# Five of seven head projections of a dilated mixer moved into seven-product block units

## The chip, the cores and the metric

The kernel runs on one core of a Trainium2 chip. The metric is the device time of one execution in microseconds (us), lower is better. A core has a matrix engine (TensorE, in the profile PE, with its weight loads as PEld), a vector engine (VectorE, DVE), an engine for functions of one argument (ScalarE, ACT), a general engine (GpSimd, POOL) and an engine that here only issues transfers (SyncE, SP). Each works through its own queue in order; semaphores order them among each other. TensorE writes to PSUM, of which the kernel uses eight banks: two under the name pj, six under the name at. All else lies in SBUF or in DRAM. Transfers (DMAs) are issued from the queues of SP, ACT and POOL and run beside the engines.

## The reference

One layer of a decoder trunk over 512 tokens and 2048 channels. The input is normalised and modulated to u, and one wide projection of u gives the columns of three token mixers (A: differential attention, B: retention, C: dilated windows) and of their gates. Of C, which the change is about, this is computed for 8 heads of width 128 and three groups (window, dilation) = (128,1), (512,4), (2048,16):

```
proj = einsum('bsd,de->bse', u, w_in)          # c_q, c_k, c_v: 3 groups x 8 heads x 128 columns each
s = einsum(qs * dh ** -0.5, kk); s = where(valid, s, -inf)     # per group and head
lse = logsumexp(s); p = exp(s - lse); o = einsum(p, vv)
o = sum over groups of softmax(lse over groups) * o
y_c = (o * silu(c_z)) @ P_c
merged = sigmoid(g_a) * y_a + sigmoid(g_b) * y_b + sigmoid(g_c) * y_c
x = x + gate(c) * (merged @ W_out), then a last rms_norm
```

All is float32. A product of two float32 matrices is made of three TensorE products of rounded parts: each operand is split into a high part (rounded, "h") and a low part (the rest, "l"), and hh, hl and lh are summed in PSUM (`mm3`, L157 to L160). The high part is a copy on ACT, the low part a subtraction, nearly always on DVE.

## The kernel before

Tokens lie on the free axis: u is held as 16 tiles of 128 channels by 512 tokens, split into `uh` and `ul`. The work runs in stages one after another: a start (modulation, normalisation, raw gate columns), a stage of block units, then mixer C with its gate phase, mixer A with its gate phase, mixer B with its gate phase, the output projection.

**A plain projection**, `proj` (L162), makes 128 columns for all 512 tokens. Its weights come in two halves of 1024 by 128 (`w_load`, a 512 KB DMA on SP; `w_half`, the ACT copy at L146 and the DVE subtraction at L147), through a ring of three buffers each for the raw, high and low parts (wr, wh, wl). Each half gives 24 products of 512 columns, 48 for a projection. A function `mid` can be called between the halves; in stage C it carries the attention work of a step before.

**A block unit**, `unit_jobs` (L555), makes 1024 columns of the same projection with the seven products of Strassen's scheme (Winograd's form) over a 2 by 2 division of tokens, channels and columns, where the direct way has eight. It is a list of 14 jobs: two each for P1, P2 and R3 ("plain" jobs, weights as they are) and eight for the four products of weight sums ("sum" jobs). A job loads 1 MB of weights to an xr tile (three buffers), in a sum job makes four additions on DVE (L592), splits it (`x_split`: ACT at L506, DVE at L507; two buffers for xh and xl), and multiplies. With `fm=True` the weights are stationary and 256 tokens move, so a job is 48 products of 256 columns and the result has channels on partitions; else it is 24 products of 512 columns. The loop at L676 loads for job i+2, splits for job i+1 and multiplies job i; the split of job i+1 needs the buffer that job i-1 leaves, so its ACT copy begins as job i begins. Nine units run: five for values (v of C's three groups, of A and of B; written to `v_dram`), four for the gates of A and B (`fm=True`; an ACT sigmoid, then written by POOL's queue). The order of this stage is that of the text where `pin` is called.

**Stage C** (L942 to L976) runs for each head seven plain projections: q and k of the three groups, and z, the gate path. Results are split from PSUM (`split` L177, `split_pairs` L196) and consumed within the head: `first_scores` (group 1: products, mask and row minimum on DVE, exp on ACT, statistics sent through DRAM), `first_turn` (seven transposes and a split), `scores(1)` and `scores(2)` (the dilated groups, which see the tokens in the order of `perm`), and, held over to the next head, `turn` (eight transposes and a split), `values` (products with v, evacuation), `weigh` on POOL and `finish`. v is loaded every second head for two heads by `v_load` (L210) through the ring of the weights. The bias of C's gate (a weighted column sum of the gate weights, 9 blocks) is built on POOL at one block or so per head by `gate_bias_load` (L707), with its own DMAs on POOL's queue, and finished by a single small product (`gate_bias_sum`, L722).

The order of the instructions on each queue outside pinned text is made by the framework's scheduler from the text's order and the times at which operands are ready, so work after a `mid` may be put before it. Buffers with `bufs=1` make a writer wait for the last reader of the old content.

Of the kernel before, what the change touches and what calls it, by code (L numbers as in the profile page):

```python
# [17 lines left out]
P = 128  # L18
S = 512
# [45 lines left out]
def hybrid_kernel(ctx, tc, x, c, w_in, w_pa, w_pb, w_pc, w_out, w_ada, b_ada, norm_w, lam,  # L65
# [32 lines left out]


# [34 lines left out]

    def w_half(src, k0, c0, rot=False, tiles=None, low=dve):

        r, h, l = tiles or w_load(src, k0, c0)
# [7 lines left out]
        else:  # L145
            act.copy(h, r)  # L146
            low.tensor_sub(l, r, h.bitcast(F32))  # L147
        return h, l

    pinned = [False]  # L150

    def pin(instr):

        if pinned[0]:
            tc.keep_in_program_order(instr)
# [40 lines left out]
    def split_pairs(pool, tag, src):  # L196

        t = pool.tile([P, 4, 2, P], F32R, tag=tag, name=tag)
        act.copy(t[:, :, 0, :], src)
        dve.tensor_sub(t[:, :, 1, :], src, t[:, :, 0, :].bitcast(F32))  # L200
        return t
# [353 lines left out]
    def unit_jobs(w, c0, put, fm=False, early=False):  # L555
# [4 lines left out]
        def pure_load(k0, cc):  # L560
            r = wxp.tile([P, 4, 512], F32, tag="xr", name="xr", bufs=3)
            nc.sync.dma_start(out=r, in_=w[k0:k0 + 512, cc:cc + 512].rearrange("(j p) c -> p j c", p=P))
            return r
# [21 lines left out]
        def sum_load(j):  # L585
            r = wxp.tile([P, 4, 512], F32, tag="xr", name="xr", bufs=3)
            for i in range(2):
                nc.sync.dma_start(out=r[:, 2 * i:2 * i + 2, :],
                                  in_=w[(i * HJ + j) * P:(i * HJ + j + 1) * P, c0:c0 + 1024]
                                  .rearrange("p (a c) -> p a c", a=2))  # L590
# [59 lines left out]
    def put_gates(g, b0):  # L650
        def put(t, half, cc):
            def f():
# [6 lines left out]


    units = [unit_jobs(w_in, c0, put_values(unit), early=unit == 3)
             for unit, c0 in ((2, C_V), (3, C_V + 1024), (4, C_V + 2048), (0, A_V), (1, B_V))]
    units += [unit_jobs(w_in, g + b0 * P, put_gates(g, b0), fm=True) for g in (G_A, G_B) for b0 in (0, 8)]
    jobs = units[1][0] + units[0][0] + units[0][1] + units[1][1]
# [26 lines left out]
    pinned[0] = False  # L691
    for f in later:
        f()
    for f in deferred:
        f()
    wx_es.close()
# [3 lines left out]
    wp_es, wp = open_pool("wp2", "left", reuse_waits="tile")  # L700
# [5 lines left out]

    def gate_bias_load(pool, db):  # L707
        br = pool.tile([P, P], F32, tag="br", name="br", bufs=2)
        for q in range(4):
            r = pool.tile([P, 4, P], F32, tag="bw", name="bw", bufs=1)  # L710
            nc.gpsimd.dma_start(out=r, in_=w_in[q * 512:(q + 1) * 512, G_C + db * P:G_C + (db + 1) * P]
                              .rearrange("(j p) c -> p j c", p=P))
            nc.gpsimd.tensor_mul(r, r, sh[:, q * 4:q * 4 + 4].unsqueeze(2).broadcast_to([P, 4, P]))
            nc.gpsimd.tensor_add(r[:, 0:2, :], r[:, 0:2, :], r[:, 2:4, :])
            if q == 0:
                nc.gpsimd.tensor_add(br, r[:, 0, :], r[:, 1, :])
            else:
                nc.gpsimd.tensor_add(r[:, 0, :], r[:, 0, :], r[:, 1, :])
                nc.gpsimd.tensor_add(br, br, r[:, 0, :])
        return br  # L720

    def gate_bias_sum(db, br):  # L722
# [83 lines left out]
    bias_todo, bias_open = list(range(NF + NM)), []  # L806

    def bias_step():
        while bias_open:
            gate_bias_sum(*bias_open.pop(0))  # L810
        bias_more()

    def bias_more():
        if bias_todo:
            db = bias_todo.pop(0)
            bias_open.append((db, gate_bias_load(cp, db)))

# [4 lines left out]
    def c_head(hd, e1, e23, st, p0):  # L822
# [3 lines left out]
        def first_scores(qh, ql, kc):  # L826
# [504 lines left out]
```

## Time and profile before

| what | us |
|---|---|
| median of 3 runs (2663.86 to 2667.76) | 2665.14 |
| the profiled execution's own time | 2663.64 |
| its span, first to last instruction | 2661.9 |
| stage of block units, first to last product, about | 723 |
| stage C up to its gate phase, about | 681 |
| mean granted TensorE clock over the span | 0.989 |

The page lists each engine's busy time; its chain of waits, followed back from the end, says which engine held the end up at each moment. Products overlap in the pipeline, so the duration of one (some 0.39 us for 512 columns) is longer than the distance from one start to the next, and the cost of a product is that distance. The answer by windows gives busy times in a chosen stretch, from the span's start.

### The profile page before, as it was taken

To read this page: it belongs to the slowest core of one execution; us is meant where nothing else is said; L and a number is where in the kernel's file an instruction comes from. 1 tells how busy PE (TensorE), PEld (TensorE's weight loads), DVE (VectorE), ACT (ScalarE), POOL (GpSimd) and SP (SyncE) were. 2 spreads that over 40 slices of the span, in tenths; PEclk is the share of its full clock that TensorE was granted. 3 is DMA by queue.
4 is the path that set the end of the run, shared out by engine and by line. 5 is a ranking of instruction groups with operands and counts; after the bars stand their busy time and mean duration, and the time that the engine had idled before them with its cause. 6 is when DMAs were issued, how large, how long until landed. Compare 5 with 4: busy or idle time off the path is not lost.

```text
span 2661.9 us, 33296 instructions
## 1 busy us (share of the span) xinstructions
PE 2568.5 (96%) x13091; PEld 2184.6 (82%) x13091; DVE 1689.0 (63%) x2427; ACT 1058.6 (40%) x1431; POOL 269.6 (10%) x271
## 2 busy tenths in 40 slices
PE   6999999999999999999999999999999989999898
PEld 5777778888999988888888888788888768878778
DVE  7994888777778754444443444357667457676674
ACT  4233433333334433233333333246666235653222
POOL 3332000000000024122214200000000000000000
PEclk9999999999999999999999999999999999999999
DMA  9776666666666655344445443542333563336862
GB/s 345 252 273 227 231 208 226 225 221 214 197 207 220 208 154 147 96 119 120 114 119 123 106 121 109 175 142 82 93 88 92 171 194 104 98 99 210 299 222 103
DMA packets 414017, 449.47 MB, mean 169 GB/s; under 512 B 24786, under 2 KB 308132, under 8 KB 412708
## 3 DMA queue, kind: packets, MB, share of 16 engines
q1 hardware_dynamic: 384388, 396.91, 47.6%
q0 software_dynamic: 9760, 33.59, 4.2%
q10 hardware_dynamic: 19712, 16.85, 1.9%
q8 instruction: 102, 1.67, 0.3%
q14 instruction: 55, 0.45, 0.1%
HBM read 406.86 MB, written 40.44 MB: 168 GB/s over the span
## 4 chain that ended last, share of the span: by engine, by line
PE 74%; DVE 11%; DMA 8%; ACT 3%; issue 2%; SPq 0%; POOL 0%; ACTq 0%; DVEq 0%
PE pj L158 15%; PE pj L160 15%; PE pj L159 15%; PE at L159 8%; PE at L160 8%; PE at L158 8%; DVE acc L318 3%; DMA gpr<-part 2%; DMA gwa<-in_w_ada_dram 1%; DVE xl L507 1%; DMA gsg<-g 1%; DMA xr<-in_w_in_dram 1%; DMA part<-gsg 1%; DMA xr<-ud 1%; DVE xr L592 1%
## 5 line engine op out<-in xcount | busy, mean ns | idle before, releaser
L158 PE MATMUL pj<-uh,wh 128*128 128x512 f32 x1552 | 611.9, 394 | 7.1 <-ACT wh L146 4.8
L160 PE MATMUL pj<-uh,wl 128*128 128x512 f32 x1552 | 608.0, 392 | 7.3 <-DVE wl L144 4.6
L159 PE MATMUL pj<-ul,wh 128*128 128x512 f32 x1552 | 606.7, 391 | 0.0
L147 DVE TENSOR_TENSOR wl<-wr,wh 128x1024 fp32r<-128x1024 f32 x226 | 287.0, 1271 | 392.0 <-ACT wh L146 364.6
L146 ACT CAST wh<-wr 128x1024 fp32r<-128x1024 f32 x228 | 239.2, 1051 | 516.7 <-PE pj L159 365.7
L506 ACT CAST xh<-xr 128x2048 fp32r<-128x2048 f32 x126 | 240.7, 1910 | 365.0 <-PE at L160 152.5
L507 DVE TENSOR_TENSOR xl<-xr,xh 128x2048 fp32r<-128x2048 f32 x126 | 288.8, 2292 | 125.4 <-ACT xh L506 124.6
L160 PEld LDWEIGHTS pj<-uh,wl 128*128 128x128 f32 x1552 | 292.5, 188 | 70.3 <-DVE wl L144 5.5
L158 PEld LDWEIGHTS pj<-uh,wh 128*128 128x128 f32 x1552 | 293.0, 189 | 65.1 <-ACT wh L146 5.0
L159 PEld LDWEIGHTS pj<-ul,wh 128*128 128x128 f32 x1552 | 292.8, 189 | 58.1
L592 DVE TENSOR_TENSOR xr<-xr 128x512 f32<-128x512 f32 x288 | 198.8, 690 | 12.3 <-DMA xr<-in_w_in_dram 5.1
L158 PE MATMUL at<-yh,wh 128*128 128x512 f32 x336 | 131.8, 392 | 5.9 <-DVE gsg L777 5.0
L159 PE MATMUL at<-yl,wh 128*128 128x512 f32 x336 | 131.5, 391 | 0.0
L160 PE MATMUL at<-yh,wl 128*128 128x512 f32 x336 | 131.5, 391 | 0.0
L160 PE MATMUL at<-fh,xl 128*128 128x256 f32 x384 | 108.9, 284 | 0.7 <-DVE xl L507 0.7
L158 PE MATMUL at<-fh,xh 128*128 128x256 f32 x384 | 108.7, 283 | 0.0
L159 PE MATMUL at<-fl,xh 128*128 128x256 f32 x384 | 108.7, 283 | 0.0
L158 PE MATMUL at<-wh,mh 128*128 128x512 f32 (+1 forms) x256 | 93.1, 369 | 6.2 <-DVE res L1252 3.8
L159 PE MATMUL at<-wl,mh 128*128 128x512 f32 (+1 forms) x256 | 94.9, 371 | 0.2
L160 PE MATMUL at<-wh,ml 128*128 128x512 f32 (+1 forms) x256 | 94.5, 369 | 0.0
L278 POOL TENSOR_TENSOR wl<-wr,wh 128x896 fp32r<-128x896 f32 x32 | 77.3, 2421 | 136.5 <-ACT wh L277 127.3
L159 PE MATMUL at<-xl,fh 128*128 128x512 f32 x224 | 88.8, 396 | 2.1 <-DVE xl L507 1.8
(419 smaller groups left out, 5035.4 us busy)
## 6 DMA issues: line engine op xcount, KB each, us to landing
wr<-in_w_in_dram SPq DMA_DIRECT2D x196, 512.0 KB, 3.9
xr<-in_w_in_dram SPq DMA_DIRECT2D x144, 512.0 KB, 4.5
xr<-in_w_in_dram SPq DMA_DIRECT2D x54, 1024.0 KB, 5.1
wa<-in_w_ada_dram SPq DMA_DIRECT2D x20, 1024.0 KB, 9.1
wr<-in_w_out_dram SPq DMA_DIRECT2D x32, 512.0 KB, 4.6
gwa<-in_w_ada_dram SPq DMA_DIRECT2D x32, 512.0 KB, 4.8
wr<-in_w_in_dram SPq DMA_DIRECT2D x32, 448.0 KB, 6.3
wb<-in_w_ada_dram SPq DMA_DIRECT2D x12, 1024.0 KB, 9.3
```

What stands on the lines that cost most here:

```text
L146: act.copy(h, r)
L147: low.tensor_sub(l, r, h.bitcast(F32))
L158: pin(nc.tensor.matmul(ps, lhsT=ah, rhs=bh, start=start, stop=False))
L159: pin(nc.tensor.matmul(ps, lhsT=ah, rhs=bl, start=False, stop=False))
L160: pin(nc.tensor.matmul(ps, lhsT=al, rhs=bh, start=False, stop=stop))
L278: nc.gpsimd.tensor_sub(l, r, h.bitcast(F32))
L318: dve.scalar_tensor_tensor(out=acc, in0=wa[:, j, :], scalar=sc[:, k:k + 1], in1=acc, op0=ALU.mult, op1=ALU.add)
L506: pin(act.copy(h, r))
L507: pin(dve.tensor_sub(l, r, h.bitcast(F32)))
L592: pin(dve.tensor_add(r[:, o, :], r[:, o, :], r[:, a, :]))
```

## The change

- The q and k of groups 1 and 2 and the q of group 3 (C_Q, C_K, C_Q+1024, C_K+1024, C_Q+2048, 1024 columns each) become five more units with `fm=True`, written to `qk_dram` by POOL's queue (`put_raw`). They stand behind the gate units; the value units of A and B move to the end.
- Stage C has two plain projections per head left: k of group 3 (C_K+2048) and z. The other five operands come back from DRAM: `first_inputs` loads straight into the tiles of the low parts, `turned` through two buffers of its own (rq), and both split from SBUF. v is loaded per head, straight into the tiles of the low parts (`head_values`), no longer through the weights' ring.
- `first_scores` of head hd+1 is called in head hd, between the halves of its z projection. `turn` of the head before and `scores(1)` stand between the halves of the k projection, `values` of the head before and `first_turn` behind it.
- The sums of the gate bias are made in the stage of units: 72 pieces, one behind every second job from job 30 on, with DMAs of 128 KB on SP and the arithmetic on POOL; the blocks wait in DRAM (`br_dram`) and `gate_bias` finishes all nine behind the last head.
- The weights of the first k projection are loaded and split while the last unit's results are evacuated (`entry`); the pool of weights is opened ahead of that. The loads of the units are pinned too.
- The broadcast of the softmax weights (`wtb`) has a buffer of its own and is issued at the end of `scores(2)`.

```diff
+    QK = [C_Q, C_K, C_Q + 1024, C_K + 1024, C_Q + 2048]
+    qk_dram = [dram.tile([8, P, S], F32, tag=f"qk{i}", name=f"qk{i}") for i in range(len(QK))]
...
+        if tiles is not None and len(tiles) == 2:
+            return tiles
...
-            act.copy(h, r)
-            low.tensor_sub(l, r, h.bitcast(F32))
+            pin(act.copy(h, r))
+            pin(low.tensor_sub(l, r, h.bitcast(F32)))
...
+    def put_raw(dst):
+        def put(t, half, cc):
+            b = cc // P
+            nc.gpsimd.dma_start(out=dst[b:b + 4, :, half * 256:half * 256 + 256].rearrange("b p t -> p b t"),
+                                in_=t.rearrange("p q (a t) -> p (q a) t", a=2))
+        return put
...
+    def bias_piece(n):
+        db, q = divmod(n, 8)
+        if q == 0:
+            bias_tiles[db] = wxp.tile([P, P], F32, tag="br", name="br")
+        br = bias_tiles[db]
+        r = wxp.tile([P, 2, P], F32, tag="bw", name="bw")
+        pin(nc.sync.dma_start(out=r, in_=w_in[q * 256:(q + 1) * 256, G_C + db * P:G_C + (db + 1) * P]
+                              .rearrange("(j p) c -> p j c", p=P)))
+        nc.gpsimd.tensor_mul(r, r, sh[:, q * 2:q * 2 + 2].unsqueeze(2).broadcast_to([P, 2, P]))
+        if q == 0:
+            nc.gpsimd.tensor_add(br, r[:, 0, :], r[:, 1, :])
+        else:
+            nc.gpsimd.tensor_add(r[:, 0, :], r[:, 0, :], r[:, 1, :])
+            nc.gpsimd.tensor_add(br, br, r[:, 0, :])
+        if q == 7:
+            nc.gpsimd.dma_start(out=br_dram[db], in_=bias_tiles.pop(db))
...
-             for unit, c0 in ((2, C_V), (3, C_V + 1024), (4, C_V + 2048), (0, A_V), (1, B_V))]
+             for unit, c0 in ((2, C_V), (3, C_V + 1024), (4, C_V + 2048))]
     units += [unit_jobs(w_in, g + b0 * P, put_gates(g, b0), fm=True) for g in (G_A, G_B) for b0 in (0, 8)]
+    units += [unit_jobs(w_in, c0, put_raw(dst), fm=True) for c0, dst in zip(QK, qk_dram)]
+    units += [unit_jobs(w_in, c0, put_values(unit)) for unit, c0 in ((0, A_V), (1, B_V))]
...
-    pinned[0] = False
+        if i >= 30 and i % 2 == 0 and (i - 30) // 2 < 8 * (NF + NM):
+            bias_piece((i - 30) // 2)
+    wx_es.close()
+    wp_es, wp = open_pool("wp2", "left", reuse_waits="tile")
+
+    loads = [w_load(w_in, half * 1024, C_K + 2048) for half in range(2)]
+    entry = []
+    for tiles in loads:
+        entry.append(w_half(w_in, 0, 0, tiles=tiles))
+        later.pop(0)()
     for f in later:
         f()
...
+    def gate_bias():
+        r = wp.tile([P, NF + NM - 1, P], F32, tag="wr", name="wr", bufs=3)
+        nc.sync.dma_start(out=r, in_=br_dram[0:NF + NM - 1].rearrange("b p c -> p b c"))
+        r2 = wp.tile([P, P], F32, tag="wr", name="wr", bufs=3)
+        nc.sync.dma_start(out=r2, in_=br_dram[NF + NM - 1])
         pc = at()
-        nc.tensor.matmul(pc[:, 0:1], lhsT=br, rhs=ones[:, 0:1], start=True, stop=True)
-        dve.tensor_copy(gbias[:, db:db + 1], pc[:, 0:1])
+        for db in range(NF + NM):
+            nc.tensor.matmul(pc[:, db:db + 1], lhsT=r[:, db, :] if db < NF + NM - 1 else r2, rhs=ones[:, 0:1],
+                             start=True, stop=True)
+        dve.tensor_copy(gbias, pc[:, 0:NF + NM])
...
+    def first_inputs(hd):
+        qh = cp.tile([P, S], F32R, tag="qh", name="qh", bufs=2)
+        ql = cp.tile([P, S], F32R, tag="ql", name="ql", bufs=2)
+        kc = cp.tile([P, 4, 2, P], F32R, tag="kc", name="kc", bufs=2)
+        qr, kr = ql.bitcast(F32), kc[:, :, 1, :].bitcast(F32)
+        nc.sync.dma_start(out=qr, in_=qk_dram[0][hd])
+        nc.sync.dma_start(out=kr, in_=qk_dram[1][hd].rearrange("p (t c) -> p t c", c=P))
...
+    def turned(i, hd):
+        r = cp.tile([P, S], F32, tag="rq", name="rq", bufs=2)
+        nc.sync.dma_start(out=r, in_=qk_dram[i][hd])
+        if i % 2 == 0:
+            return split(cp, "q", r, scale=dh_scale, view=perm, bufs=2)
+        return split_pairs(cp, "kc", perm(r), bufs=2)
+
+    def head_values(hd):
+        vs = []
+        for g in range(3):
+            vh = cp.tile([P, NT, P], F32R, tag=f"v{g}h", name="vh")
+            vl = cp.tile([P, NT, P], F32R, tag=f"v{g}l", name="vl")
+            src = v_dram[2 + g][:, hd * P:(hd + 1) * P]
+            r = vl.bitcast(F32)
+            nc.sync.dma_start(out=r, in_=src.rearrange("(i r) c -> i r c", r=4) if g
+                              else src.rearrange("(t p) c -> p t c", p=P))
+            act.copy(vh, r)
+            dve.tensor_sub(vl, r, vh.bitcast(F32))
+            vs.append((vh, vl))
+        return vs
+
     left = [None, None]
+    head = c_head(0)
+    first = first_inputs(0)
+    second = turned(2, 0), turned(3, 0)
     for hd in range(8):
...
+        def opening(turn_left=left[0]):
+            if turn_left is not None:
+                turn_left()
+            if hd == 0:
+                first_scores(*first[0], first[1])
+            scores(1, *second[0], second[1])
+
+        ps = proj(C_K + 2048 + hd * P, tiles=entry or (None, None), mid=opening)
+        entry = None
+        if left[1] is not None:
+            left[1]()
+        first_turn()
+        third = turned(4, hd), split_pairs(cp, "kc", perm(ps), bufs=2)
+        vs = head_values(hd)
+        if hd < 7:
+            first = first_inputs(hd + 1)
+
+        def closing():
+            scores(2, *third[0], third[1])
+            if hd < 7:
+                head[0](*first[0], first[1])
+
+        sz = silu(cp, proj(C_Z + hd * P, mid=closing), bufs=1)
+        if hd < 7:
+            second = turned(2, hd + 1), turned(3, hd + 1)
...
-    bias_step()
+    gate_bias()
     gate_phase(G_C, w_pc, "first", left=left)
```

More of the change, by code (lines that the diff above doesn't have):

```diff
@@ L950, in hybrid_kernel @@
-        e23 = cp.tile([P, 4, 256], F32, tag="e23", name="e23")
-        first_scores, first_turn, scores, turn, values, weigh, finish = c_head(hd, e1, e23, st, p0)
-        cq, ck = C_Q + hd * P, C_K + hd * P
-        ps = proj(cq + 1024, mid=lambda: first_scores(*q, kc))
-        q2 = split(cp, "q", ps, scale=dh_scale, view=perm)
-        ps = proj(ck + 1024, mid=first_turn)
-        kc2 = split_pairs(cp, "kc", perm(ps))
-        ps = proj(cq + 2048, mid=lambda: scores(1, *q2, kc2))
-        q3 = split(cp, "q", ps, scale=dh_scale, view=perm)
@@ L959, in hybrid_kernel @@
-        kc3 = split_pairs(cp, "kc", perm(proj(ck + 2048)))
-        if hd == 4:
-            bias_more()
-        if hd % 2 == 0:
-            vs = [v_load(cp, 2 + g, hd * P, f"v{g}", strided=g > 0) for g in range(3)]
-        sz = silu(cp, proj(C_Z + hd * P, mid=lambda: scores(2, *q3, kc3)))
+        first_scores, first_turn, scores, turn, values, weigh, finish = head
+        head = c_head(hd + 1)
+        def opening(turn_left=left[0]):
[4 more added lines that the diff above has]
+            scores(1, *second[0], second[1])
```

89 lines of the change are left out of this document (36 added, 53 removed).

## The prediction

> **What bounds the kernel now.** I read the page first: busy shares, then the chain of waits.
>
> ```profile
> span 2661.9 us, 33296 instructions
> ...
> PE 2568.5 (96%) x13091; PEld 2184.6 (82%) x13091; DVE 1689.0 (63%) x2427; ACT 1058.6 (40%) x1431; POOL 269.6 (10%) x271
> ...
> PE 74%; DVE 11%; DMA 8%; ACT 3%; issue 2%; SPq 0%; POOL 0%; ACTq 0%; DVEq 0%
> ```
>
> TensorE is busy for 96% of the span and holds 74% of the chain, so the question is stage by stage whether it idles. Next came the answer by windows: the units, stage C, two heads of C, a head of A, a head pair of B, one gate unit.
>
> ```profile
> core 0: us, PE busy (x) PEld busy (x) DVE busy (x) ACT busy (x) POOL busy (x), PEclk, DMA share, GB/s
> 238.64:961.33 722.69, 711.91 (x4369) 640.59 (x4367) 572.62 (x568) 281.21 (x187) 25.37 (x35) 0.99 0.64 214
> 961.33:1642.62 681.29, 676.04 (x3238) 567.52 (x3237) 290.85 (x529) 240.97 (x386) 158.20 (x196) 0.99 0.45 120
> 1070.17:1154.86 84.69, 84.69 (x412) 71.31 (x411) 35.06 (x67) 28.65 (x47) 17.57 (x22) 1.00 0.39 106
> 1154.86:1239.54 84.68, 84.68 (x411) 71.30 (x411) 38.18 (x69) 31.58 (x50) 17.62 (x22) 1.00 0.45 124
> 1791.60:1830.88 39.28, 38.97 (x185) 32.20 (x185) 27.50 (x56) 24.43 (x42) 0.00 (x0) 1.00 0.28 81
> 2199.68:2251.96 52.28, 51.00 (x236) 42.12 (x236) 37.69 (x59) 32.62 (x60) 0.00 (x0) 1.00 0.30 90
> 660.00:740.67 80.67, 80.67 (x674) 80.67 (x673) 61.83 (x59) 34.02 (x23) 3.01 (x4) 1.00 0.63 205
> ```
>
> A head of C is 84.7 us of unbroken TensorE work at full clock, with DVE busy for 37 us; a gate unit is 80.67 us, also unbroken. So both stages are bound by TensorE, and what counts is products times their distance. TensorE's waits in stage C are two rows:
>
> ```profile
> PE pj L158 <- ACT wh L146: 4.8, 1, 4.8
> PE at L869 <- DVE kc L200: 0.4, 1, 0.4
> ```
>
> Stage C has nothing to win from better overlap but that entry of 4.8 us. The gain must come from fewer product columns.
>
> **The change part by part. First, the products.** The timeline of TensorE gives distances, that of DVE the period of a unit:
>
> ```profile
> 1106.00 0.45 PE L158 MATMUL pj<-uh,wh 128*128 128x512 f32 x1
> ...
> 1127.62 0.40 PE L160 MATMUL pj<-uh,wl 128*128 128x512 f32 x1
> ```
>
> ```profile
> 800.37 0.28 PE L160 MATMUL pj<-uh,xl 128*128 128x256 f32 x1
> 800.49 0.28 PE L158 MATMUL pj<-uh,xh 128*128 128x256 f32 x1
> ```
>
> ```profile
> 660.24 1.41 DVE L580 TENSOR_TENSOR c<-p,at 128x512 f32<-128x512 f32 x2 [0.94 <-PE at L160]
> 740.91 1.41 DVE L580 TENSOR_TENSOR c<-p,at 128x512 f32<-128x512 f32 x2 [0.89 <-PE at L160]
> ```
>
> Between the first two lines lie 96 products of 512 columns, 95 distances: 21.62 / 95 = 0.2276 us, so a projection of 48 costs 10.92 us. Removed: 5 projections by 8 heads, 40 x 10.92 = 436.9 us. Added: five units of the gates' form. Each has 14 jobs of 48 products, 672 x 0.120 = 80.6 us, which the period of the real unit confirms (740.91 - 660.24 = 80.67): 403.4 us. The difference is **-33.5 us**. A seventh less work would have given an eighth of 437, 55 us; the 256-column product takes 0.120 us where half of a 512-column one is 0.114, and that eats the rest.
>
> The Trainium skill ("TensorE: Matmul & The Clock Gate", section on the back-to-back issue gap) puts the distance at N/2.4 + 2.5 ns, that is 216 and 109 ns; by it the estimate would be 40 x 48 x 0.2158 - 5 x 672 x 0.1092 = 47 us of gain. The rows above are longer in both forms, and more so in the small one, so the measurement decides.
>
> **The entry to stage C.** Now it goes like this:
>
> ```profile
> 961.21 0.28 PE L160 MATMUL at<-uh,xl 128*128 128x256 f32 x1
> 966.26 0.79 PE L158 MATMUL pj<-uh,wh 128*128 128x512 f32 x1 [4.77 <-ACT wh L146]
> ...
> 970.24 0.45 PE L160 MATMUL pj<-uh,wl 128*128 128x512 f32 x1
> ```
>
> A pause of 4.8 us, then eight distances that take 3.98 us where 8 x 0.2276 = 1.82 are due: 7.0 us lost. With the first k weights split beside the last unit the pause goes. What is late next are head 0's own operands: their tiles lie where the last unit's buffers were, so loads begin at its end, land in some 3.9 us (below) and need ACT and DVE, while the first half projection covers 24 x 0.2276 = 5.5 us. I take 2 us of loss out of bounds 0 and 7: **-5 us**.
>
> **Short heads.** A head of C keeps two projections: 84.69 - 5 x 10.92 = 30.1 us of TensorE work. Its DVE and ACT load comes from the two-head window:
>
> ```profile
> L147 DVE TENSOR_TENSOR wl<-wr,wh 128x1024 fp32r<-128x1024 f32 x29 | 40.2, 1386 | 73.6 <-ACT wh L146 67.5 <-PE at L901 6.1
> ...
> L146 ACT CAST wh<-wr 128x1024 fp32r<-128x1024 f32 x28 | 29.4, 1051 | 82.9 <-PE pj L159 71.8 <-issue 7.8 <-DVE v2l L220 2.6
> ```
>
> DVE per head is (35.06 + 38.18) / 2 = 36.6 us, of which 20.1 are weight splits; four of fourteen stay, 5 us: 21.5 us, 71% of 30.1. ACT: 30.1 - 10 x 1.05 = 19.6 us, 65%. Splits of q, k and v keep their number or volume; they read SBUF instead of PSUM, at nothing. The heads of A and B run with such loads (27.50 of 39.28; 37.69 of 52.28), and TensorE idles 0.31 and 1.28 us there: 0.2 to 0.7 us per 30. Here the attention chain has half the distance between its steps, so I take 1.0 us a head: **+8 us**, bounds 2 and 36 (the third rival). Through the six at buffers go 13 tiles a head, as before, in 30 us.
>
> **Added DMAs and waits.** Per head 1.25 MB of q and k come back and 2 MB of weights stay, some 4 MB with v in 30 us, 133 GB/s; the gate unit moves 205 GB/s with TensorE unbroken, so nothing; without that cover a landing, 3.9 us a head. `put_raw` takes the place that `put_gates` has on POOL's queue, without its ACT step: nothing; its tiles are wanted again a unit, 80 us, later. On SP the pinned piece loads stand ahead of the next xr load and wait for POOL's arithmetic of the piece before, 11 us old: nothing, and with that cover gone a piece's 2 us. The broadcast of `wtb` waits on POOL for a DRAM round trip, behind it the statistics of the next head, wanted a head later: nothing. Bias products at the end take two of three ring buffers from the gate phase: between 0 and one load and split, 6 us; I take **+1**.
>
> **The bias sums beside the units.** They are now where DVE is fullest. Two rows of DVE and one of POOL show what POOL does to a subtraction with both inputs in SBUF; then POOL's arithmetic, and the rhythm of sum jobs in a gate unit:
>
> ```profile
> 1232.01 1.22 DVE L147 TENSOR_TENSOR wl<-wr,wh 128x1024 fp32r<-128x1024 f32 x1 [3.35 <-ACT wh L146]
> ...
> 1237.44 2.84 DVE L147 TENSOR_TENSOR wl<-wr,wh 128x1024 fp32r<-128x1024 f32 x1 [3.61 <-ACT wh L146]
> ```
>
> ```profile
> 1237.89 1.30 POOL L934 TENSOR_TENSOR sz<-sz,wtb 128x512 f32<-128x512 f32 x1
> ```
>
> ```profile
> L714 POOL TENSOR_TENSOR bw<-bw 128x256 f32<-128x256 f32 x36 | 32.5, 902 | 2.8
> ...
> L718 POOL TENSOR_TENSOR bw<-bw 128x128 f32<-128x128 f32 x27 | 15.5, 574 | 2.1
> ```
>
> ```profile
> 697.41 2.29 DVE L507 TENSOR_TENSOR xl<-xr,xh 128x2048 fp32r<-128x2048 f32 x1 [0.69 <-ACT xh L506]
> 699.62 2.87 DVE L592 TENSOR_TENSOR xr<-xr 128x512 f32<-128x512 f32 x4
> 703.17 2.29 DVE L507 TENSOR_TENSOR xl<-xr,xh 128x2048 fp32r<-128x2048 f32 x1 [0.68 <-ACT xh L506]
> ```
>
> ```profile
> 706.99 1.90 ACT L506 CAST xh<-xr 128x2048 fp32r<-128x2048 f32 x1 [3.85 <-PE at L159]
> ```
>
> The subtraction takes 1.22 us alone and 2.84 us around a POOL product of 1.30: it was held for at least all of that. A piece is one product of 128x256 and two additions of 128x128, 0.90 + 2 x 0.57 = 2.05 us, every second job. A sum job lasts 703.17 - 697.41 = 5.76 us, DVE needs 2.29 + 2.87 = 5.16 of it, and its split ends at 705.46, 1.5 us before TensorE turns to the next job at 706.99. Much of POOL's time will fall into the 0.68 us that DVE waits for ACT and into plain jobs, where DVE is half idle. I take **+3 us** over nine units; bounds 0 and 31 (nine units, eight jobs, (5.16 + 2.05 / 2 - 5.76) = 0.43 us, no reserve).
>
> The sum: -33.5 - 5 + 8 + 1 + 3 = -26.5 us, on the execution's own 2663.6: 2637.1. The runs' median lies 1.5 us above that execution; with it **2638.6 us**.
>
> **The rivals.** *The lock makes the units DVE-bound.* The Trainium skill ("SBUF — State Buffer", section on who interferes with whom) states that a DVE instruction with two SBUF inputs and a GpSimd instruction that reads SBUF exclude each other for a whole instruction. The row of 2.84 us agrees. If DVE pays each piece in full, two sum jobs need 2 x 5.16 + 2.05 = 12.37 us where TensorE takes 11.52; a unit falls 3.4 us behind, less the reserve of 1.5, times nine: 17 us instead of 3, 2653 us. Against it: pieces fall into plain jobs in six of fourteen.
>
> *The v loads block the weights (slower).* `head_values` loads into single buffers that `values` of the head before reads. If SP issues in the text's order, the weights of z stand behind that wait. Here is `values` of one head, from first product to the next projection, then `first_turn` and three rows on the loads:
>
> ```profile
> 1067.01 0.28 PE L916 MATMUL at<-p,v1h 128*128 128x256 f32 x1
> ...
> 1070.17 0.44 PE L158 MATMUL pj<-uh,wh 128*128 128x512 f32 x1
> ```
>
> ```profile
> L858 PE MATMUL at<-ident,e 128*128 128x128 f32 x7 | 0.9, 272 | 0.0
> ```
>
> ```profile
> SPq L132 <- DVE wl L147: 462.3, 88, 9.3
> ```
>
> ```profile
> L132 SPq DMA_DIRECT2D wr<-in_w_in_dram x28: 367/368/374, 1070.8 to 1233.3; - x28
> ```
>
> ```profile
> wr<-in_w_in_dram SPq DMA_DIRECT2D x196, 512.0 KB, 3.9
> ```
>
> Weights would be asked for 3.2 us after the k projection and five other loads, 0.37 each, and be there 3.9 + 1.05 + 1.23 us later: 11.2 us, of which `values` and `first_turn` (0.9) cover 4.1: 7 us a head, 56 in all, 2695 us. It decides from 26.5 / 8 + 1 = 4.3 us a head. Against it: now a weight load is issued when a ring buffer comes free (88 waits for the split), two or three halves ahead of use, and the scheduler lets ready work pass.
>
> *The short head idles at its handovers.* A head has five (turn to `values`, the k split to `scores(2)`, its exp to `turn`, the second splits to `scores(1)`, `first_scores` to `first_turn`). The longest comparable waits stand in B:
>
> ```profile
> PE at L993 <- DVE sqs L988: 1.9, 2, 0.9
> ```
>
> Five such, 4.5 us a head instead of 1: 28 us more, 2667 us, no change.
>
> **Chances.** Forecast 0.63, from 2624 (entry and stalls at nothing) to 2650. Lock 0.12, 2650 to 2660. Idle handovers 0.12, 2655 to 2672. Blocked weights 0.13, 2672 to 2700. The range 2624 to 2664 leaves out the last, some of the third and a little below. Faster by over 0.2% (5.3 us, about what a measurement of this kernel can tell) are the first two and a third of the third: 0.79; within it, half of the third, 0.06; slower 0.15.
>
> **What would show it.** Stage of units: 403 us longer, no new DVE waits at xl L507 beyond a few us; longer L592 and L507 beside POOL mean the lock. Heads of C: about 31 us from `turn` to `turn`; 37 with TensorE waiting for ACT wh L146 mean blocked weights, waits at products of attention mean handovers. Entry: a pause under 3 us. Wrong would be above all a unit whose period is not 80.7 us, or a head over 34.

## The result, and the profile after

The changed kernel takes 2693.4 us (median of 4 runs, 2690.3 to 2697.8) where the kernel before takes 2666.5 in the same comparison: ratio 1.0099, 95% interval 1.0075 to 1.0123. It is slower by about 1%; 26.5 us less were forecast. The profiled execution took 2697.8 us. The head of its page, busy times by engine and the chain of waits:

```profile
span 2696.0 us, 36917 instructions
...
PE 2563.4 (95%) x14531; PEld 2246.5 (83%) x14531; DVE 1912.5 (71%) x2646; ACT 1130.1 (42%) x1453; POOL 293.5 (11%) x336
...
PE 67%; DVE 13%; DMA 13%; ACT 4%; issue 3%; SPq 0%; ACTq 0%; DVEq 0%
```

Nothing there looks alarming: TensorE is busy for 95% instead of 96%, with 5.1 us less of busy time. But DMA has gone from 8% to 13% of the chain, and TensorE from 74% to 67%. Where that happens is told by landmarks. The timeline of TensorE, first after: the last product of the units, the first product of stage C, the first transpose of `turn` of the first and of the last head.

```profile
1372.49 0.39 PE L166 MATMUL at<-xh,ul 128*128 128x512 f32 x1
1372.71 0.39 PE L164 MATMUL pj<-uh,wh 128*128 128x512 f32 x1
...
1414.01 0.33 PE L931 MATMUL at<-ident,e 128*128 128x128 f32 x1 [4.95 <-ACT e L913]
...
1678.03 0.60 PE L931 MATMUL at<-ident,e 128*128 128x128 f32 x4
```

and the two transposes before the change:

```profile
1055.25 0.60 PE L901 MATMUL at<-ident,e 128*128 128x128 f32 x4
...
1647.63 0.60 PE L901 MATMUL at<-ident,e 128*128 128x128 f32 x4
```

The last product of the units stood at 961.21 before (shown in the prediction). So the difference of the two spans, 2696.0 - 2661.9 = 34.1 us, falls into four pieces:

| piece | before | after | difference | forecast |
|---|---|---|---|---|
| start and units, to their last product | 961.2 | 1372.5 | +411.3 | +406.4 |
| from there to the first `turn` | 94.0 | 41.5 | -52.5 | -58.6 |
| seven periods, first `turn` to the eighth | 592.4 | 264.0 | -328.4 | -375.2 |
| from the eighth `turn` to the end | 1014.3 | 1018.0 | +3.7 | +1 |

The forecast column applies the prediction's terms to each piece: 403.4 + 3; five projections (54.6), 5 of entry, and 1 of stall; seven periods of 31.1 (30.1 and a stall of 1.0) against 84.69; the bias products. Of 60.6 us between forecast and profile, 46.8 lie in the seven periods of the short heads: 264.0 / 7 = 37.7 us each instead of 31.1. The last piece is mostly spread: it lies between 1014 and 1024 us in the other profiles of this study.

The answer by windows for the units, the first head, the seven periods, and one of them (columns as in the prediction; the clock is the number behind the POOL bracket):

```profile
238.75:1372.49 1133.74, 1118.70 (x7729) 1045.59 (x7727) 903.92 (x862) 431.60 (x282) 185.71 (x271) 0.99 0.66 220
1372.49:1414.01 41.52, 35.08 (x170) 27.34 (x168) 26.31 (x64) 21.72 (x34) 2.85 (x4) 1.00 0.75 194
1414.01:1678.03 264.02, 231.58 (x1173) 199.08 (x1173) 157.74 (x393) 142.19 (x282) 18.76 (x21) 0.91 0.55 123
...
1489.50:1526.75 37.25, 32.97 (x169) 28.55 (x167) 23.01 (x57) 20.11 (x40) 2.60 (x3) 0.91 0.56 123
```

In the seven periods TensorE idles for 264.02 - 231.58 = 32.4 us, and the granted clock falls to 0.91; in the other stages it is 0.98 to 1.00. Who makes it idle is told by its waits in that window (for whom, us in total, times, longest; of the 5.1 us at L931, 5.0 are the wait that ends at the window's start):

```profile
PE at L897 <- DVE kc L206: 28.6, 6, 7.5
PE at L931 <- ACT e L913: 5.1, 2, 5.0
PE at L164 <- ACT kc L982: 2.0, 1, 2.0
```

28.6 of it is one place, the first product of `scores(2)`, which waits for the split of the third k. That is the second of the five handovers in the prediction's third rival. TensorE never waits for weights in a projection, so the rival with the blocked weights isn't what happened; that its 2695 us is nearly the time measured is chance. Why the split is late shows in the queue of the engine ahead of DVE, ACT, in one period:

```profile
1493.49 1.07 ACT L205 CAST p<-at 128x512 fp32r<-128x512 f32 x2
1506.57 0.63 ACT L979 ACTIVATE qh<-ql 128x512 fp32r<-128x512 f32 x1 [12.00 <-DMA ql<-qk]
1507.10 1.03 ACT L159 CAST wh<-wr 128x1024 fp32r<-128x1024 f32 x1
1508.04 0.58 ACT L205 CAST kc<-pj 128x512 fp32r<-128x512 f32 x1
```

ACT stands still for 12 us, not for the third k (whose products had ended) but for the load of the next head's q (L979, in `first_inputs`). The scheduler put that copy ahead of the copy of the third k, which it cannot pass. And that load is late because SP had come late to issue it. SP's queue (the second number is the time from the first issue's start to the end of the last one of the row):

```profile
1486.23 6.96 SPq L988 DMA_DIRECT2D rq<-qk  x3
1494.00 6.07 SPq L136 DMA_DIRECT2D wr<-in_w_in_dram  x2
1500.16 1.32 SPq L977 DMA_DIRECT2D ql<-qk  x1
1501.53 0.54 SPq L978 DMA_DIRECT2D kc<-qk  x1
```

Two weight loads hold SP from 1494.00 to 1500.07, the second alone for 4.93 us, where the prediction had 0.37 us for an issue. (The three of the first row took 0.3 us each, with a pause between them.) Over the seven periods, the DMA issues (count, KB each, median us to landing), then q's time on SP (min/median/max in ns):

```profile
wr<-in_w_in_dram SPq DMA_DIRECT2D x23, 512.0 KB, 5.7
...
ql<-qk SPq DMA_DIRECT2D x6, 256.0 KB, 10.0
...
bounce<-st ACTq DMA_DIRECT2D x7, 4.0 KB, 11.4
```

```profile
L977 SPq DMA_DIRECT2D ql<-qk x6: 319/4207/7055, 1418.4 to 1611.0; - x6
```

A quarter of a megabyte takes 10 us to land, counted from the start of its issue, and the issue alone takes 4.2 us at the median. One suspect stands out: the smallest transfer, 4 KB, takes longest. It is the first group's row statistics, `st1` of 128x8, written to DRAM as 1024 pieces of 4 bytes (L869), issued at 1488.8 in the period above, 5 us ahead of the stretch in which SP is stuck. It was there before, and as slow (11.4 us), but then q and k were not loaded and the weights were asked for halves ahead of use.

What the other transfers do until this write has landed, the windows show. First the kernel after, where the write lands at 1500.2; then the kernel before, where one was issued at 1509.38 and had landed by 1521.14, when POOL issued the read of it. The last two numbers are the DMA share and GB/s:

```profile
1493.20:1500.20 7.00, 7.00 (x47) 6.37 (x46) 4.61 (x14) 1.37 (x3) 0.00 (x0) 1.00 0.88 100
1500.20:1505.70 5.50, 5.50 (x29) 4.65 (x28) 0.00 (x0) 0.00 (x0) 2.01 (x2) 1.00 1.07 279
```

```profile
1514.40:1521.10 6.70, 6.70 (x34) 5.60 (x33) 2.46 (x4) 1.91 (x3) 0.00 (x0) 1.00 0.23 22
1521.10:1524.10 3.00, 3.00 (x15) 2.48 (x14) 0.00 (x0) 0.00 (x0) 0.74 (x1) 1.00 0.91 280
```

In both kernels the loads crawl while the write is on its way, at 100 and 22 GB/s, and run at about 280 GB/s right behind it. Before the change a 512 KB weight load, issued at 1513.99, took 9.8 us for it where the median is 3.9, and TensorE was busy all the time. The 512 KB broadcast of `wtb` from POOL's queue, which in the kernel after stands at the same place, is slowed too: 8.8 us to landing at the median of that run, 5.0 before the change.

Last, the idle time costs twice. The window of the idle time, and that of the products behind it:

```profile
1507.00:1510.60 3.60, 0.00 (x0) 0.00 (x0) 3.13 (x5) 3.60 (x8) 0.00 (x0) 0.90 0.02 5
1510.67:1516.50 5.83, 5.83 (x24) 5.54 (x25) 4.77 (x9) 1.97 (x4) 0.00 (x0) 0.50 0.83 223
```

After 4.3 us of idling the clock is 0.50 for 5.8 us: 2.9 us more are lost. 4.3 + 2.9 = 7.2 is what this period (37.25 us) has over 30.1. The pause of 2.0 us in the list of waits (L164), which ends at 1437.61, has its slow stretch too:

```profile
1438.21:1441.62 3.41, 3.29 (x13) 3.18 (x14) 3.38 (x7) 2.37 (x6) 0.00 (x0) 0.50 0.29 78
```

The Trainium skill ("TensorE: Matmul & The Clock Gate", section on HAM oscillation) says that idle gaps of TensorE over some 3.4 us bring the clock down to half. The trace agrees for the long pauses, but not on the length that it takes: here 2.0 us were enough, and the measurement decides.

### The profile page after: what moved, and what is told of

Same layout as the page of the kernel before. It is cut to its first block, busy times and chain, and to the rows that moved or that the text cites. A ratio compares the mean times of both kernels' runs of the same rounds, so it can differ in the third digit from the quotient of the medians.

```text
span 2696.0 us, 36917 instructions
## 1 busy us (share of the span) xinstructions
PE 2563.4 (95%) x14531; PEld 2246.5 (83%) x14531; DVE 1912.5 (71%) x2646; ACT 1130.1 (42%) x1453; POOL 293.5 (11%) x336
## 4 chain that ended last, share of the span: by engine, by line
PE 67%; DVE 13%; DMA 13%; ACT 4%; issue 3%; SPq 0%; ACTq 0%; DVEq 0%
PE at L166 11%; PE at L165 11%; PE at L164 11%; PE pj L164 10%; PE pj L165 10%; PE pj L166 10%; DVE acc L324 4%; DMA gpr<-part 2%; DMA ql<-qk 2%; DVE xl L513 2%; DMA gwa<-in_w_ada_dram 2%; DMA xr<-in_w_in_dram 1%; DMA gsg<-g 1%; DVE xr L598 1%; DVE wl L160 1%
## 5 line engine op out<-in xcount | busy, mean ns | idle before, releaser
L513 DVE TENSOR_TENSOR xl<-xr,xh 128x2048 fp32r<-128x2048 f32 x196 | 452.0, 2306 | 194.1 <-ACT xh L512 192.5
L166 PE MATMUL pj<-uh,wl 128*128 128x512 f32 x912 | 360.1, 395 | 5.7 <-DVE wl L157 3.1
L164 PE MATMUL pj<-uh,wh 128*128 128x512 f32 x912 | 363.6, 399 | 0.8 <-ACT wh L156 0.8
L165 PE MATMUL pj<-ul,wh 128*128 128x512 f32 x912 | 359.5, 394 | 0.0
L598 DVE TENSOR_TENSOR xr<-xr 128x512 f32<-128x512 f32 x448 | 329.8, 736 | 18.5 <-DMA xr<-in_w_in_dram 7.0
L164 PE MATMUL at<-fh,xh 128*128 128x256 f32 x864 | 245.2, 284 | 0.0
L164 PEld LDWEIGHTS pj<-uh,wh 128*128 128x128 f32 x912 | 174.6, 191 | 35.5 <-ACT wh L156 1.3
L166 PEld LDWEIGHTS at<-fh,xl 128*128 128x128 f32 x864 | 166.2, 192 | 5.6 <-DVE xl L513 5.5
L165 PEld LDWEIGHTS at<-fl,xh 128*128 128x128 f32 x864 | 166.3, 192 | 0.0
L164 PEld LDWEIGHTS at<-fh,xh 128*128 128x128 f32 x864 | 166.2, 192 | 0.0
L165 PE MATMUL at<-ul,xh 128*128 128x256 f32 x576 | 163.0, 283 | 0.0
L164 PE MATMUL at<-uh,xh 128*128 128x256 f32 x576 | 163.0, 283 | 0.0
L166 PE MATMUL at<-uh,xl 128*128 128x256 f32 x576 | 163.0, 283 | 0.0
L164 PE MATMUL at<-yh,wh 128*128 128x512 f32 x336 | 132.7, 395 | 6.4 <-DVE gsg L809 6.4
```

Source lines behind the costliest of these rows:

```text
L164: pin(nc.tensor.matmul(ps, lhsT=ah, rhs=bh, start=start, stop=False))
L165: pin(nc.tensor.matmul(ps, lhsT=ah, rhs=bl, start=False, stop=False))
L166: pin(nc.tensor.matmul(ps, lhsT=al, rhs=bh, start=False, stop=stop))
L513: pin(dve.tensor_sub(l, r, h.bitcast(F32)))
L598: pin(dve.tensor_add(r[:, o, :], r[:, o, :], r[:, a, :]))
```

## Experiments

The theories: **A**, the 4-byte writes make the loads behind them late; **B**, the mere volume asked for at that place does; **C**, the order in ACT's queue turns a late load into idle time of TensorE; and for the units, **D**, POOL's sums for the bias hold VectorE up. All ratios are to the kernel before, run beside each. "Period" is the mean from `turn` to `turn` over seven.

| run | us | ratio, 95% interval | period |
|---|---|---|---|
| the change | 2693.4 | 1.0099, 1.0075 to 1.0123 | 37.7 |
| rows of statistics (e1) | 2659.3 | 0.9973, 0.9961 to 0.9984 | 31.8 |
| ACT's order (e2) | 2674.8 | 1.0037, 1.0024 to 1.0050 | 35.3 |
| bias sums left out (e4) | 2685.8 | 1.0069, 1.0053 to 1.0085 | 36.5 |
| e1 and e2 (e5) | 2647.9 | 0.9928, 0.9909 to 0.9947 | 31.2 |
| rows, later (h1) | 2647.5 | 0.9935, 0.9915 to 0.9955 | 31.6 |
| rows, later, and ACT's order (b0) | 2638.4 | 0.9902, 0.9890 to 0.9915 | 30.2 |
| b0, scores back (g1) | 2634.7 | 0.9885, 0.9861 to 0.9909 | 29.9 |
| the change, scores back (u1) | 2694.7 | 1.0107, 1.0094 to 1.0120 | 36.1 |
| b0, bias on VectorE (b1) | 2662.0 | 0.9983, 0.9975 to 0.9992 | 30.2 |
| b0, bias at plain jobs (f1) | 2642.8 | 0.9913, 0.9893 to 0.9933 | 30.3 |
| before, with rows (c1) | 2666.3 | 1.0000, 0.9992 to 1.0009 | 84.8 |
| the change, 4-byte write later in the text (k1) | 2687.4 | 1.0077, 1.0052 to 1.0102 | 37.0 |

**e1, the statistics as rows** (A against B):

```
-            nc.scalar.dma_start(out=bounce.rearrange("s (a p) -> p s a", p=P), in_=st1)
+            tp = at()
+            nc.tensor.transpose(tp[0:8, 0:P], st1.rearrange("p s a -> p (s a)"), ident)
+            rows = cp.tile([8, P], F32, tag="rows", name="rows", bufs=2)
+            dve.tensor_copy(rows, tp[0:8, 0:P])
+            nc.scalar.dma_start(out=bounce.rearrange("s (a p) -> (s a) p", p=P), in_=rows)
```

> The changed kernel, with the first group's row statistics (128x8) turned on TensorE to 8x128 and sent to DRAM as 8 rows of 512 bytes, in place of 1024 writes of 4 bytes. Theory A (the scattered 4-byte write, 11.4 us to land, stands in front of the loads of q and k on the DMA engines, and ACT waits for them): the write lands in under 4 us; q's load to landing falls from 13.6 us at most to under 7; TensorE's waits for kc at the second scores fall from 29.2 us in 7 to under 10, turn to turn from 37.4 to about 33.5 us, and the kernel takes 2660 to 2670 us. Theory B (the volume asked for at that place, 1.5 MB within 10 us, makes them late): the write is shorter, the loads stay as late, and the kernel takes 2685 to 2695 us. Each head also gets one transpose and one copy more, under 0.5 us.

2659.3 us, 34 less by the medians. In its seven periods, TensorE's waits, ACT's longest, and q's time on SP:

```profile
PE at L870 <- ACT e L865: 8.1, 5, 2.5
PE at L165 <- DVE kc L987: 3.4, 1, 3.4
...
ACT qh L983 <- DMA ql<-qk: 27.6, 5, 7.0
...
L981 SPq DMA_DIRECT2D ql<-qk x6: 531/624/1011, 1421.1 to 1582.2; - x6
```

The wait for the third k is gone from the list, where under 10 us were expected, and issuing q takes 0.6 us instead of 4.2 at the median. The broadcast of `wtb` is still there and lands in 4.2 us, so it alone was not the cause. A holds, with nothing else changed in the loads. The new wait at L870 is the price of the edit itself: the transpose of the statistics waits for the last exponential. ACT still waits 27.6 us for q, where it waited 73.6 us in the changed kernel; so loads remain that are not early, and here a part for B is left.

**c1, the same rows in the kernel before** (the control: five lines as in e1, but the rows lie in an unused corner of `e1`).

> The kernel before the change, with the rows of statistics (8 rows of 512 bytes, turned on TensorE) in place of the 1024 writes of 4 bytes. If the scattered write costs only where loads stand close ahead of their use (in the long head weights are asked for two or three halves ahead, and q and k are never loaded), nothing is gained: 2664 to 2670 us, the transposes' 8 x 0.3 us included. If the write is slow work that any kernel pays for, 2640 to 2655 us.

Ratio 1.0000 within 0.1%. Yet the loads do change. The time to landing of the weight loads (L132) from the second head of stage C to its end, first in the kernel before, then in c1:

```profile
DMA to landing us min/median/max: 3.6/3.9/10.0
```

```profile
DMA to landing us min/median/max: 3.7/3.8/5.6
```

The slowest takes 5.6 us instead of 10.0, and nothing is gained, because in the long heads even the slow ones were asked for early enough. So the slow write is not a cost in itself; it costs what is loaded close ahead of its use behind it.

**e2, ACT's order** (C):

```
-        vs = head_values(hd)
-        if hd < 7:
-            first = first_inputs(hd + 1)
+        with tc.issue_after(last_copy[0]):
+            vs = head_values(hd)
+            if hd < 7:
+                first = first_inputs(hd + 1)
```

(`last_copy[0]` is the ACT copy of the third k's split; only ACT's instructions of the block are put behind it.)

> The changed kernel, with ACT's copies of the values and of the next head's q and k made to stand behind ACT's copy of the third k in its queue (loads are issued where they were). Theory C (a late load costs TensorE time only because ACT's copy of the next q stands ahead of the copy of the third k in a queue that keeps its order): waits for kc at the second scores fall from 29.2 us in 7 to under 8, though q still lands as late; 2660 to 2672 us. Rival (what is late is the data of several copies, and the first scores of the next head, just behind, need that q anyway): TensorE's wait moves from the second scores to the first scores right behind them, and the kernel takes 2680 to 2693 us.

2674.8 us, between the two. In the seven periods:

```profile
PE at L899 <- DVE gpr L953: 11.2, 4, 4.1
PE at L933 <- ACT e L915: 3.8, 2, 3.6
PE at L899 <- DVE kc L208: 3.1, 2, 2.7
```

The wait for the third k (L208 here) falls from 28.6 to 3.1, but at the same product (L899) TensorE now waits for the evacuation of `values` (L953 on DVE, behind L952 on ACT), whose ACT copy stands behind the late q. So C is right and pays half: with a late load, an order only chooses what stands behind it. The rival named the wrong place, the first scores, but the right kind of result.

**e5, e1 and e2 together.**

> Both edits, of the rows of statistics and of ACT's order. If both theories, A and C, name the same stall, the gain is that of the better one alone and little more (2658 to 2668 us); if the late loads cost a second stall of their own, for example at the next head's first scores or at the weights, the two gains add and the kernel takes 2645 to 2658 us.

2647.9 us: e2's edit still gains 11 us on top of e1's. The loads with the rows are not early enough for ACT's order to be of no account.

**b0, the rows turned later.** As e5, with the transpose, its copy and the two transfers in a function that is called behind `first_turn`, a third of a head on; `rows` lies in the corner of `e1` that holds nothing.

> The version with the rows of statistics and ACT's order, with the rows turned a head later, behind the first group's transposes, so that TensorE doesn't wait for the last exponential there (3.5 us in 7 waits). If nothing waits for the rows at the new place, those waits go and it takes 2643 to 2648 us; if the weights of the second scores wait for the rows' way through DRAM (about 4 + 4 us), it takes 2650 to 2665 us.

2638.4 us, below what was expected. The seven periods by windows, and all of TensorE's waits in them:

```profile
1408.78:1619.90 211.12, 210.82 (x1178) 182.75 (x1178) 158.52 (x399) 144.59 (x281) 19.17 (x21) 1.00 0.55 153
...
PE at L907 <- DVE kc L208: 0.2, 1, 0.2
```

211.12 / 7 = 30.2 us a period, of which TensorE idles 0.3 us in all seven; the clock is 1.00. This is the change with its fault mended: 1% faster than the kernel before.

**h1, the later rows without ACT's order.**

> The changed kernel with the rows of statistics turned on TensorE behind the first group's transposes, as in the fastest version, but with ACT's copies in the order of the changed kernel. If q now lands in time because nothing stands in front of its load, ACT's order costs nothing any more: 2636 to 2643 us. If the order is needed too (the two loads with the 128 KB or more around them still land behind the third k), it lies where the first version of the rows was beside the one with both edits, some 10 us above the fastest: 2645 to 2655 us.

2647.5 us: the order is needed too, 9 us here, 11 between e1 and e5. The two edits add up in part: alone they gain 34 and 19 us, together 45.

**k1, the 4-byte write later**: the function of b0, with `st1` written as it is.

> The changed kernel with the 1024 writes of 4 bytes kept, but issued a third of a head later, behind the first group's transposes. If it is only the collision of this write with the loads of q and k that costs (both stand at the middle of the k projection in the changed kernel), moving it recovers most of what replacing it does: 2640 to 2660 us. If the write holds up whatever stands behind it, and now meets the weights of z and the values, the kernel stays slow, with TensorE's waits at another place: 2675 to 2700 us.

2687.4 us, and nothing learnt: the write moved in the text alone. Nothing holds it to TensorE's work, so the scheduler put it back to where it was, right behind the exponentials, and the waits are the old ones:

```profile
1489.66 0.37 ACTq L873 DMA_DIRECT2D bounce<-st  x1
...
PE at L901 <- DVE kc L206: 27.8, 6, 6.1
```

Whether moving the write would have done stays open. In b0 the transpose ties it to TensorE's order, so there it did move.

**u1 and g1, first scores back in their own head**, on the changed kernel and on b0:

```
-            if hd == 0:
-                first_scores(*first[0], first[1])
+            first_scores(*first[0], first[1])
...
-            if hd < 7:
-                head[0](*first[0], first[1])
```

> The changed kernel with one part undone: each head's first scores stand at the middle of its own k projection again, not at the middle of the z projection of the head before. If the order ahead is needed in the short head, TensorE waits for the eight exponentials before the first group's transposes (DVE some 2.5 us, ACT 1.3 us of table load and 8 times 0.5 us, against the 5.4 us of the second half of the projection and the scores of the second group): 1 to 3 us a head, 2700 to 2715 us, with the waits for kc at the second scores unchanged. If the stall of the changed kernel comes from that order (the next q and k are loaded early for it), the waits for kc shrink and it takes 2670 to 2685 us. If neither, 2690 to 2697 us.

> The fastest version so far, with each head's first scores at the middle of its own k projection again. In the changed kernel this order made no difference (2694.7 against 2693.4 us), because ACT stood still for the late loads either way. If the order ahead is what a short head needs once ACT runs freely, TensorE now waits for the exponentials at the first group's transposes: 1 to 4 us a head over the 30.1 us from turn to turn, 2646 to 2670 us. If the rest of the head covers them, 2636 to 2642 us.

Neither differs from its partner: 1.0107 against 1.0099, 0.9885 against 0.9902, intervals overlapping. In u1 the waits for the third k are gone, as in the second case, but the time isn't better; TensorE's idle time now stands at `turn`, behind exponentials that are late as ACT waits for k (6.9 of the 28.2 us end at the start of the window):

```profile
PE at L931 <- ACT e L913: 28.2, 15, 6.9
...
ACT kc L982 <- DMA kc<-qk: 43.2, 6, 7.8
```

In g1 the same window shows no wait of TensorE at all. A part of the change, the first scores a head ahead, buys nothing that can be measured.

**e4, the bias sums left out** (D; 126 additions and 72 products on POOL):

> The changed kernel, with POOL's sums for the gate's bias left out but for one addition in eight (the gate's bias is then not the reference's; the loads stay). If the units are 8 us longer than 80.67 us each because VectorE's sums wait for POOL's use of the shared port, the seven-block units come to 80.7 us each, the units end 7 to 8 us sooner, and the kernel takes 2684 to 2687 us. If it is the loads of the bias or something else of the units, nothing changes: 2691 to 2695 us.

2685.8 us, 7.6 below the change by the medians, though the two intervals overlap. The profiles are clearer: the start of the last c rows (DVE, L586) of the units, and VectorE's sums over all units (count, busy, mean ns), each first in the change, then in e4:

```profile
1317.43 0.69 DVE L586 TENSOR_TENSOR c<-p,at 128x512 f32<-128x512 f32 x1 [0.52 <-PE at L166]
...
L598 DVE TENSOR_TENSOR xr<-xr 128x512 f32<-128x512 f32 x448 | 329.8, 736 | 18.5 <-DMA xr<-in_w_in_dram 7.0
```

```profile
1310.07 1.37 DVE L586 TENSOR_TENSOR c<-p,at 128x512 f32<-128x512 f32 x2 [0.52 <-PE at L166]
...
L598 DVE TENSOR_TENSOR xr<-xr 128x512 f32<-128x512 f32 x448 | 309.9, 692 | 18.1 <-DMA xr<-in_w_in_dram 6.9
```

The units end 7.4 us sooner without POOL's work, and a sum of VectorE takes 692 ns instead of 736, with the same waits ahead of it (18.5 and 18.1 us). D holds; the price is 7 us, not 3.

**b1 and f1, other places for the bias sums**, on b0. b1 has two VectorE instructions for POOL's three; f1 asks for eight pieces between a unit's job 12 and job 5 of the next, counted from 0:

```
+        for a in range(2):
+            s = sh[:, q * 2 + a:q * 2 + a + 1]
+            if q == 0 and a == 0:
+                dve.tensor_scalar_mul(br, r[:, 0, :], s)
+            else:
+                dve.scalar_tensor_tensor(out=br, in0=r[:, a, :], scalar=s, in1=br, op0=ALU.mult, op1=ALU.add)
```

```
-        if i >= 30 and i % 2 == 0 and (i - 30) // 2 < 8 * (NF + NM):
-            bias_piece((i - 30) // 2)
+        if i >= 26 and (i - 28) % 14 in (13, 12, 0, 1, 2, 3, 4, 5) and pieces:
+            bias_piece(pieces.pop(0))
```

> The same, and the gate's bias summed by two VectorE instructions of 128x128 for each piece in place of POOL's three. If POOL's use of the shared port is what makes the units 7.6 us longer and VectorE has room for 2 x 0.25 us in every second job, the units end 6 to 8 us sooner and it takes 2636 to 2642 us, what was predicted for the change. If VectorE has no such room, the units are no shorter: 2643 to 2655 us.

> The fastest version so far (rows of statistics turned later, ACT's order), with the 72 pieces of the gate's bias asked for from the twelfth job of a unit to the fifth of the next (eight a unit, so that POOL works on them beside plain jobs, where VectorE is half idle), in place of one at every second job. If VectorE loses time only where its sums meet POOL, most of the 7.6 us of the units comes back: sum jobs at 80.7 us a unit, 2631 to 2635 us. If one piece a job is too close for POOL or for the loads (a piece's buffer comes free only behind its sums, and the load of the next stands on SP ahead of the unit's own), the units grow instead: 2640 us and over. If the lock costs as much wherever POOL works, nothing changes: 2636 to 2641 us.

Both fail. b1 takes 2662.0 us, 24 more than b0 and more than either case had; VectorE's new work and what it waits for:

```profile
L692 DVE SCALAR_TENSOR_TENSOR br<-bw,sh,br 128x128 f32<-128x128 f32 x135 | 47.0, 348 | 33.9 <-DMA bw<-in_w_in_dram 32.7
```

Besides 47 us of work it stands 32.7 us for the bias loads, in front of the sums that TensorE needs. f1 (2642.8) is not distinguishable from b0; its units are no shorter, although its sums are:

```profile
L600 DVE TENSOR_TENSOR xr<-xr 128x512 f32<-128x512 f32 x448 | 317.9, 710 | 20.9 <-DMA xr<-in_w_in_dram 9.6
```

They take 710 ns instead of 736, more than half of what e4 won, and it gains nothing. So the mean length of the sums isn't what sets the units' time. That VectorE is half idle in plain jobs is no cover for POOL, and why isn't settled.

## Why the prediction was wrong

- **The products, -33.5.** Right in size (seven products for eight are an eighth less, as the 55 us there has it, not a seventh). Without POOL's work (e4) the units take 403.9 us more than before, where 403.4 were forecast; a period of b0, with all of the change's products and nearly none of its idle time, takes 30.2, where 30.1 were. b0 as a whole takes 28.2 us less than the kernel before (2666.7 to 2638.4). That this is within 2 us of the forecast of 26.5 is in part luck: POOL cost more than forecast and the stalls, once mended, less.
- **POOL's lock, +3.** That POOL's work costs time in the units was right and the size wrong: about 7 (e4), inside the bounds of 0 and 31. The 3 was taken, not worked out. VectorE's sums are held up (e4), but how that comes to 7 us is open (f1).
- **The entry, -5.** The pause of 4.8 us went, as the first product of stage C follows the last of the units after 0.22 us. But head 0 lost more than the 2 us taken: its first `turn` came after a wait of 4.95 us, and the piece to that point is 6 us over the forecast. Most of that is the late loads again: in b0 the same piece takes 36.6 us instead of 41.5, with 35.4 forecast.
- **Added DMAs, nothing.** This is the step that failed. It compared a mean rate, 133 GB/s in the short heads with 205 in a gate unit, and concluded that the loads of q and k are hidden; "without that cover a landing, 3.9 us a head" was its other end. But a mean rate says nothing on when one load is there: q took 10.0 us at the median to land and 4.2 to be issued, at a DMA share of 0.55 (e1 and the windows around the 4-byte write show what stood in front of it). That write was already in the kernel before, and the prediction gave its effect on other loads no price.
- **Short heads, +8.** So the stall was mis-sized too: 1.0 us a head by the idle time of the heads of A and B, with bounds of 2 and 36 us for all eight. The seven periods alone hold 264.0 - 7 x 30.1 = 53 us, 7.6 each. Work per engine and distance of the attention steps, from which the 1.0 was argued, were no error: in b0 and g1 TensorE idles less than 0.1 us a head. "A head over 34" was named as what would make the prediction wrong.
- **The rivals.** The third, idle handovers, with a chance of 0.12 and 4.5 us a head, came nearest: it named the place, but not the cause, a late load ahead in ACT's queue, and its 2667 us is 26 too low. It is one handover of the five, the k split to `scores(2)`, at 28.6 / 6 = 4.8 us a wait; missed was the second loss, the slow products after it, 2.9 of the 7.2 us in the period shown and some 21 of the 53 in all seven (TensorE is busy for 231.58 us there, for 210.82 in b0). The second rival gave nearly the time that was measured and is refuted: TensorE doesn't wait for the weights of z.

The range (2624 to 2664) held the mended change but not the change as it is.

## What to carry to other kernels

When a stage is shortened, list each transfer that is issued in it with its time to landing, also those that cost nothing so far: a slow one that long work covered (here 11.4 us for 4 KB) becomes the wait of the short stage. A copy that waits for a load must not stand in an in-order queue ahead of a copy that the main engine needs now, and where the load can be late the order and the load are both worth mending: here 34 and 19 us alone, 45 together. Idle gaps of TensorE have to be priced with the slow products that can follow them, here behind a gap of 2.0 us already.

## What had not been expected of the hardware

Writing 128x8 numbers as 1024 pieces of 4 bytes took 11.4 us to land and, in the changed kernel, kept SP's queue for 4.2 us at the median with the next q's load; as 8 rows of 512 bytes it left that at 0.6 us. The Trainium skill ("DMA: Bandwidth & Descriptors", Specifications) gives 512 bytes as the least transfer for line rate. The runs agree as far as they go, with pieces of 4 and of 512 bytes; what they add is that loads from other queues crawl until such a write has landed (22 and 100 GB/s, then 280). By what means it holds them up, no run here shows.

A pause of TensorE of 2.0 us was followed by 3.4 us at a clock of 0.50; one of 2.2 us in e1 was not, so the length of the pause alone doesn't decide it.
